# Queries as plain fp32 products, the first head ahead of the rows and the other heads beside them

## The chip, the cores and the metric

The kernel runs on one core of a Trainium2 chip. Its time is device time in microseconds. Before the change the median of three runs is 1752.78 us (1751.76 to 1754.2). A profile is one execution, recorded by the hardware profiler; times inside it are from the start of its span. TensorE, VectorE, ScalarE, Gpsimd and SyncE appear in it as PE (PEld for its weight loads), DVE, ACT, POOL and SP.

## The reference

Two layers over x of 256 tokens and width 1024. Layer 0 mixes tokens by window attention with a gated spatial unit, layer 1 by average pools of four widths. After each mixer stands the part that fills most of the time and that the change touches, a product-key memory of 16384 experts:

```python
q = (xb @ w_q).reshape(n, PEER_HEADS, 2, PEER_DHALF)
s = jnp.einsum('thpk,pnk->thpn', q, sub_keys).astype(jnp.float32)
s_top, i_top = lax.top_k(s, PEER_TOPK)
cand_s = s_top[:, :, 0, :, None] + s_top[:, :, 1, None, :]
cand_i = i_top[:, :, 0, :, None] * PEER_NKEYS + i_top[:, :, 1, None, :]
best_s, best_pos = lax.top_k(cand_s.reshape(n, PEER_HEADS, -1), PEER_TOPK)
idx = jnp.take_along_axis(cand_i.reshape(n, PEER_HEADS, -1), best_pos, axis=-1)
gate = jax.nn.softmax(best_s, axis=-1)
u = jnp.take(down, idx, axis=0)
act = jax.nn.gelu(jnp.einsum('thkd,td->thk', u, xb))
v = jnp.take(up, idx, axis=0)
return jnp.einsum('thk,thkd->td', (gate * act).astype(v.dtype), v)
```

Each token has 8 heads. Per head two query halves of 128 are scored against 128 keys each, the best 16 of each half give 256 sums, and the best 16 of these name 16 experts. Each expert has a row `down` and a row `up` of 1024 floats.

## The kernel before

Channels lie on the 128 partitions in the first part of a layer: `xT` is x transposed, 8 blocks (kb) of 128 channels by 256 tokens. `peer_rows(l)` does the memory of layer l. Its work is cut into 16 **units**: one head for one half of the tokens (128 tokens on the partitions). A unit has 16 **rows**: row k is one gather, a `DMA_INDIRECT` on Gpsimd's queue (L1018) that fetches for each of the 128 tokens its k-th expert, `down` and `up` side by side, 8 KB a token. Rows live in a ring of RING = 12 slots; `fetch` issues a gather when the next slot is free and the unit has been chosen.

Ahead of the rows stand the queries. `norm_split` makes the normed activations in two parts, `xH` (rounded to fp32r) and `xL` (the rest); both, and their sum `hq` made on Gpsimd, occupy three ring slots until the last query. The weights `w_q` come as 16 blocks of 512 KB through a stream of three tiles (`raw`) on SP's queue; each block is split in halves into `sH` (a cast on ScalarE, L105) and `sL` (a subtraction on VectorE, L108). A product is then three fp32r passes, hi by hi, hi by lo and lo by hi (L317 to L319; for head 0, L340 to L343). Two blocks make a head's queries `qT`; `scores` (L1040) multiplies them by the keys, and a copy makes `sc`. `rows_of` turns `hq` into token rows `h2`.

`choose` is the choice of one unit on VectorE, a generator of some 21 steps: top 16 of each half, 256 sums, top 16 of these, expert numbers `eid`, gates by a softmax (Exp on ScalarE). `advance` takes steps of it: 4 after each query block, only for heads before the present one, so that choices stand between the splits of later heads. After the last query the row loop begins: per row a product with `h2`, summed to one number per token (L1102), and 2 steps of choices; per BATCH = 4 rows a Gelu, the gate (`cr`, L1089), four diagonal matrices `dgr` on ScalarE (L1076) and 16 passes on PE that add `up` rows to four banks (L1079). The weights of a batch are made after the first product of the next (`todo`). After its adding a row's slot is free. In layer 0 the loop also multiplies 56 blocks of modulation weights (`md`, 512 KB each, two tiles), one for each fourth row from row 16; they follow `w_q` in the same stream.

When all gathers are out, `after_rows` prepares the pool mixer between the last addings; `pool_shift` sums rows by products with ones, of fp32r parts. Then the residual is added, the pool mixer runs, and layer 1 repeats `peer_rows`. In these parts the order of the code is the order on each engine.

## Time and profile before

| | us |
|---|---|
| median of three runs | 1752.78 |
| profiled execution | 1751.43 |
| its span | 1749.4 |
| PE busy | 1352.9 (77%) |
| DVE busy | 1197.8 (68%) |
| ACT busy | 466.0 (27%) |
| POOL busy | 741.6 (42%) |
| first gather, layer 0 / layer 1 | 236.78 / 1052.56 |
| first product with a row, layer 0 / layer 1 | 269.69 / 1086.74 |
| gathers' share of 16 DMA engines over the span | 74.3% |

The kernel moves 622.52 MB. PE's busy time is modelled from pipelined matmuls, so 77% does not say how near it is to its peak. The granted clock is a share of 2.4 GHz. A stretch tells more than the span: its GB/s, its busy times and its clock say what limits it, and the idle time before an instruction names what ended it.

### The profile page before, as it was taken

Reading aid. Unit: us, or ns where it says so; the run is one execution under the profiler, and the core shown is the slowest. Engines: PE = TensorE matmul, PEld = TensorE weight load, DVE = VectorE, ACT = ScalarE, POOL = GpSimd, SP = SyncE. Lnnn points to the kernel's source line nnn. Section 1 sums busy time; section 2 is a strip of 40 time slices with the busy share of each in tenths; the row PEclk is TensorE's granted clock in tenths of the full one; section 3 lists DMA queues with packets and bytes.
Section 4 is the critical chain, followed back from the end, with each engine's and each line's share of the span. In section 5 each row is a group of like instructions: output and inputs, shape, how many; then the busy total and the mean of one; then the engine's idle time right before and its main releaser. Section 6 shows DMA issues by size and latency. Waiting matters only on the chain. (4 is left out here: it accounts for less than half of the span.)

```text
span 1749.4 us, 15727 instructions
## 1 busy us (share of the span) xinstructions
PE 1352.9 (77%) x4148; PEld 691.8 (40%) x4148; DVE 1197.8 (68%) x2910; ACT 466.0 (27%) x1176; POOL 741.6 (42%) x632
## 2 busy tenths in 40 slices
PE   7988897677767677767777797877877887777776
PEld 3865793233223233223233387333333333333333
DVE  6987768877787776555554377877777775545443
ACT  3555553222222121111111353222222222111112
POOL 3535433443444434444444133544444454544442
PEclk8987998988888978988888899899998898999899
DMA  7434578999999999999999328799999999999993
GB/s 291 164 109 158 170 280 323 419 419 419 418 419 418 419 418 418 419 419 419 419 419 414 135 86 342 321 419 420 419 419 420 419 420 420 420 420 420 418 420 124
DMA packets 97867, 622.52 MB, mean 356 GB/s; under 512 B 11250, under 2 KB 11762, under 8 KB 31860
## 3 DMA queue, kind: packets, MB, share of 16 engines
q0 software_dynamic: 73728, 536.90, 74.3%
q1 hardware_dynamic: 23328, 83.82, 12.9%
q8 instruction: 34, 0.56, 0.1%
q10 hardware_dynamic: 724, 0.80, 0.1%
q14 instruction: 53, 0.43, 0.1%
HBM read 620.44 MB, written 1.05 MB: 355 GB/s over the span
## 5 line engine op out<-in xcount | busy, mean ns | idle before, releaser
L1079 PE MATMUL ps_big<-row,dgr 128*128 128x512 f32 x2048 | 1033.4, 664 | 340.3 <-ACT dgr L1076 340.3
L1018 POOL DMA_INDIRECT row<-in_DU,eid x512 | 609.6, 1191 | 801.7 <-PE ps_big L1079 537.1
L1102 DVE SCALAR_TENSOR_TENSOR row<-row,h 128x1024 f32<-128x1024 f32 x512 | 627.2, 1225 | 419.4 <-DMA row<-in_DU,eid 407.8
L1079 PEld LDWEIGHTS ps_big<-row,dgr 128*128 128x128 f32 x2048 | 424.2, 212 | 948.1 <-issue 504.8
L1076 ACT ACTIVATE dgr<-cf,cr 128x128 f32<-128x128 f32 x512 | 164.0, 390 | 276.9 <-DVE cr L1089 275.2
L1108 ACT ACTIVATE actr<-actr 128x4 f32<-128x4 f32 x128 | 26.3, 205 | 701.0 <-DVE row L1102 700.8
L108 DVE TENSOR_TENSOR sL<-raw,sH 128x512 fp32r<-128x512 f32 x75 | 57.8, 798 | 30.7 <-ACT sH L105 24.9
L884 DVE SCALAR_TENSOR_TENSOR md<-md,crowb 128x1024 f32<-128x1024 f32 x56 | 68.1, 1216 | 0.0
L317 PE MATMUL ps_a<-row,sH 128*128 128x256 f32 x224 | 65.3, 291 | 2.3 <-ACT sH L105 1.4
L318 PE MATMUL ps_a<-row,sH 128*128 128x256 f32 x224 | 63.1, 282 | 1.0 <-issue 1.0
L319 PE MATMUL ps_a<-row,sL 128*128 128x256 f32 x224 | 63.5, 283 | 0.5 <-DVE sL L108 0.4
L105 ACT CAST sH<-raw 128x512 fp32r<-128x512 f32 x84 | 49.2, 619 | 24.5 <-DMA raw<-in_w_q 10.9
L511 PE MATMUL ps_big<-sH,hH 128*128 128x256 f32 x128 | 38.4, 306 | 8.6 <-ACT sH L105 6.1
L317 PEld LDWEIGHTS ps_a<-row,sH 128*128 128x128 f32 x224 | 42.8, 191 | 4.1 <-ACT qTp L1051 2.1
L319 PEld LDWEIGHTS ps_a<-row,sL 128*128 128x128 f32 x224 | 42.7, 191 | 1.7 <-DVE sL L108 1.1
L318 PEld LDWEIGHTS ps_a<-row,sH 128*128 128x128 f32 x224 | 42.8, 191 | 0.7 <-issue 0.7
L1102 DVE DVE_READ_ACCUMULATOR row<-row,h 128x1 f32 x512 | 42.2, 82 | 0.0
L512 PE MATMUL ps_big<-sL,hH 128*128 128x256 f32 x128 | 38.2, 301 | 2.6 <-DVE sL L108 2.5
L1001 ACT ACTIVATE gater<-best,z 128x16 f32<-128x16 f32 x32 | 9.8, 308 | 106.8 <-DVE z L1000 106.7
L513 PE MATMUL ps_big<-sH,hL 128*128 128x256 f32 x128 | 37.2, 296 | 0.1
L1001 ACT ACT_TABLE_LOAD x28 | 35.9, 1283 | 0.5
L1108 ACT ACT_TABLE_LOAD x28 | 35.9, 1283 | 0.4
(265 smaller groups left out, 1315.6 us busy)
## 6 DMA issues: line engine op xcount, KB each, us to landing
md<-in_modT SPq DMA_DIRECT2D x56, 512.0 KB, 7.9
raw<-in_w_q SPq DMA_DIRECT2D x32, 512.0 KB, 3.3
raw<-in_modT SPq DMA_DIRECT2D x19, 512.0 KB, 4.7
row<-in_DU,eid POOLq DMA_INDIRECT x512, 18.5
pro<-in_modT SPq DMA_DIRECT2D x11, 512.0 KB, 3.7
pro<-in_modA SPq DMA_DIRECT2D x8, 512.0 KB, 6.7
raw<-in_in_w SPq DMA_DIRECT2D x8, 512.0 KB, 4.4
pro<-in_in_w SPq DMA_DIRECT2D x6, 512.0 KB
```

Source lines behind the costliest of these rows:

```text
L105: k.nc.scalar.copy(hi, src)
L108: eng.tensor_sub(lo, src, hi)
L317: nc.tensor.matmul(ps, lhsT=hi[:, i], rhs=xh[:, kb], start=(first and i == 0), stop=False)
L318: nc.tensor.matmul(ps, lhsT=hi[:, i], rhs=xl[:, kb], start=False, stop=False)
L319: nc.tensor.matmul(ps, lhsT=lo[:, i], rhs=xh[:, kb], start=False, stop=(last and i == 3))
L884: self.nc.vector.scalar_tensor_tensor(raw, raw, 1.0, crow, op0=OP.mult, op1=OP.mult, accum_out=self.m[:, l, j:j + 1])
L1001: nc.scalar.activation(g, best, AF.Exp, bias=z[:, 0:1], scale=1.0, accum_out=z[:, 1:2])
L1018: nc.gpsimd.indirect_dma_start(r, None, a[f"DU{l}"], bass.IndirectOffsetOnAxis(ap=eid[:, tt, h, k:k + 1], axis=0))
L1076: nc.scalar.activation(dg, self.ident, AF.Copy, scale=cw[:, tt, s:s + 1])
L1079: nc.tensor.matmul(acc[2 * tt + hf], lhsT=dg, rhs=r[:, D + 512 * hf:D + 512 * hf + 512], start=(s == 0), stop=(s == P - 1))
L1102: nc.vector.scalar_tensor_tensor(r[:, :D], r[:, :D], 1.0, h2[:, tt], op0=OP.mult, op1=OP.mult, accum_out=act[:, tt, s:s + 1])
L1108: nc.scalar.activation(act[:, tt, s], act[:, tt, s], AF.Gelu_apprx_tanh)
```

## The change

Queries become plain fp32 products of the unsplit `w_q` tiles with `hq`, which VectorE and ScalarE make directly; a product is two passes on PE. No ring slot is taken for them and the ring has 13 slots. Head 0 is multiplied first, its scores follow, then the queries of head 1; units 0 and 1 are chosen in one piece, with 12 further steps of unit 2, 56 steps in all, ahead of the row loop. Heads 2 to 7 are multiplied in the row loop, two products at every second row (`asks`), and ScalarE's copies of queries and scores are issued one such ask later (`late`). A unit is taken up as soon as its head's scores are there. The `md` blocks have a stream of their own. The last unit's batches are 4, 4, 4, 2, 1, 1. The pool's sums are fp32 products.

```diff
-RING = 12
+RING = 13
...
+    def take(self):
+
+        i = self.pos[0]
+        self.load_ahead()
+        self.pos = (i + 1, 0)
+        return self.raw[i], i
+
+    def give(self, i):
+        self.release(i)
+        self.load_ahead()
...
-    def dense_items(self, l):
...
+    def later_items(self):
+        a = self.a
+        self.pro_end = len(self.st.items)
+        for l in range(2):
+            for j in range(16):
+                self.st.add(a["w_q"][l, j], lambda raw: None)
         for n in range(56):
             lj = (0, 40 + n) if n < 8 else (1, n - 8)
-            st.add(a["modT"][30 + n], lambda raw, lj=lj: self.mod_dot(lj, self.crow)(raw), "md")
-        self.dense_items(1)
+            self.sm.add(a["modT"][30 + n], lambda raw, lj=lj: self.mod_dot(lj, self.crow)(raw), "md")
...
-        st.ahead(4)
-        self.norm_split(self.rin.finish(), self.gcol, self.m[:, l, 24:32], xH, xL, self.xT)
+        st.load_ahead()
+        r = self.rin.finish()
         for kb in range(KB):
-            nc.gpsimd.tensor_add(hq[:, kb], xH[:, kb], xL[:, kb])
+            nc.vector.scalar_tensor_tensor(hq[:, kb], self.xT[:, kb], self.gcol[:, kb:kb + 1], r,
+                                           op0=OP.mult, op1=OP.mult)
+            nc.scalar.activation(hq[:, kb], hq[:, kb], AF.Identity, bias=self.m[:, l, 24 + kb:25 + kb], scale=1.0)
...
-            while steps > 0 and at[0] < len(units) and units[at[0]][1] < ready:
+            while steps > 0 and at[0] < len(units) and units[at[0]][1] in scs:
...
+        def query(ps, w, kb):
+            nc.tensor.matmul(ps[:, :T], lhsT=w[:, kb * P:(kb + 1) * P], rhs=hq[:, kb], start=(kb == 0),
+                             stop=(kb == KB - 1))
+
+        def queries(h):
+
             qT = tk.tile([P, 2, T], F32, name="qTp", bufs=2)
+            late = None
             for p in range(2):
-                ps = first[p] if h == 0 else self.tile_mm(xH, xL)
...
+                ps = self.bank("a")
+                w, i = st.take()
+                for kb in range(KB):
+                    query(ps, w, kb)
+                    if kb == 1 and late:
+                        late()
+                    if kb % 2:
+                        yield
+                st.give(i)
+                late = lambda ps=ps, p=p: nc.scalar.copy(qT[:, p], ps[:, :T])
+            late()
+            yield
+            late = scores(h, qT)
+            yield
+            late()
+
+        qT = tk.tile([P, 2, T], F32, name="qTp", bufs=2)
+        banks = [self.bank("a") for _ in range(2)]
+        blocks = [st.take() for _ in range(2)]
+        for kb in range(KB):
+            for ps, (w, _) in zip(banks, blocks):
+                query(ps, w, kb)
+        for p in range(2):
+            st.give(blocks[p][1])
+            nc.scalar.copy(qT[:, p], banks[p][:, :T])
+        scores(0, qT)()
+        second = queries(1)
+        for tt in range(2):
+            for hf in range(2):
+                rows_of(tt, hf)
+            for _ in range(28):
+                advance(1)
+                if tt == 0:
+                    next(second, None)
+        for _ in second:
+            pass
+        asks = (1 for h in range(2, 8) for _ in queries(h))
...
         for n, (tt, h) in enumerate(units):
             while at[0] <= n:
-                advance(1, 8)
-            for k0 in range(0, 16, BATCH):
-                for k in range(k0, k0 + BATCH):
+                next(asks, 0)
+                advance(1)
+            k0 = 0
+            for m in (BATCH,) * (16 // BATCH) if n < 15 else (BATCH,) * (16 // BATCH - 1) + (2, 1, 1):
+                for k in range(k0, k0 + m):
...
-                    advance(2, 8)
+                    if i % 2 == 0:
+                        next(asks, 0)
+                    advance(2)
...
-            for q in range(2):
-                nc.tensor.matmul(ps, lhsT=self.ones_r, rhs=self.sph[q], start=(q == 0), stop=(q == 1))
+            nc.tensor.matmul(ps, lhsT=self.ones, rhs=self.sp[:, 2 * hf:2 * hf + 2].rearrange("p g e -> p (g e)"),
+                             start=True, stop=True)
```

VectorE at the opening of layer 0, before: `nh` and `row` are the norm and the low part of the activations, `sL` the low parts of weights, `v` and `ix` the first top 16.

```order
L308 SCALAR_TENSOR_TENSOR row<-nh,m,row 128x256
L299 SCALAR_TENSOR_TENSOR nh<-xT,gcol,ps_w 128x256
L308 SCALAR_TENSOR_TENSOR row<-nh,m,row 128x256
L108 TENSOR_TENSOR sL<-raw,sH 128x512 x5
L954 MAX v<-sc 128x8
L956 MAX_INDEX ix<-v,sc 128x8
L958 MATCH_REPLACE wkt<-v,sc 128x128
L960 MAX v<-wkt 128x8
L108 TENSOR_TENSOR sL<-raw,sH 128x512 x2
L962 MAX_INDEX ix<-v,wkt 128x8
L954 MAX v<-sc 128x8
L956 MAX_INDEX ix<-v,sc 128x8
```

And in the changed kernel, from the norm on.

```order
L225 SCALAR_TENSOR_TENSOR ry<-rt_2002,rz 128x2
L932 SCALAR_TENSOR_TENSOR hq<-xT,gcol,ps_w 128x256 x8
L943 MAX v<-sc 128x8
L945 MAX_INDEX ix<-v,sc 128x8
L947 MATCH_REPLACE wkt<-v,sc 128x128
L949 MAX v<-wkt 128x8
L951 MAX_INDEX ix<-v,wkt 128x8
L943 MAX v<-sc 128x8
L945 MAX_INDEX ix<-v,sc 128x8
L947 MATCH_REPLACE wkt<-v,sc 128x128
L949 MAX v<-wkt 128x8
```

The splits are gone from between the steps of the choice, and the norm has 8 instructions.

PE at the end of the queries of layer 0, before: the last fp32r passes, the scores of head 7, and all addings of rows.

```order
L317 MATMUL ps_a<-row,sH 128x256
L318 MATMUL ps_a<-row,sH 128x256
L319 MATMUL ps_a<-row,sL 128x256
L1040 MATMUL ps_w<-keys,qTp 128x128 x4
L1079 MATMUL ps_big<-row,dgr 128x512 x512
```

And now from the first query on: `hq,raw` are queries, `cf,hq` the turning of `hq` into rows, `row,dgr` the addings.

```order
L1039 MATMUL ps_a<-hq,raw 128x256 x16
L1029 MATMUL ps_w<-keys,qTp 128x128 x4
L939 MATMUL ps_a<-cf,hq 128x128 x8
L1039 MATMUL ps_a<-hq,raw 128x256 x16
L1029 MATMUL ps_w<-keys,qTp 128x128 x4
L939 MATMUL ps_a<-cf,hq 128x128 x8
L1039 MATMUL ps_a<-hq,raw 128x256 x4
L1100 MATMUL ps_big<-row,dgr 128x512 x8
L1039 MATMUL ps_a<-hq,raw 128x256 x4
L1100 MATMUL ps_big<-row,dgr 128x512 x8
L1039 MATMUL ps_a<-hq,raw 128x256 x4
```

Queries of heads 2 to 7 stand between the addings, four products after each four rows.

SP's queue from the first w_q load on, before (`md` are modulation blocks).

```order
L70 DMA raw<-in_w_q 128x1024 x16
L70 DMA md<-in_modT 128x1024 x56
L70 DMA raw<-in_w_q 128x1024 x3
L1165 DMA row<-in_pool_w 128x2048
L1169 DMA row<-in_pm 128x1088
```

The same stretch of SP's queue now.

```order
L70 DMA raw<-in_w_q 128x1024 x7
L70 DMA md<-in_modT 128x1024 x2
L70 DMA raw<-in_w_q 128x1024 x2
L70 DMA md<-in_modT 128x1024 x3
L70 DMA raw<-in_w_q 128x1024
L70 DMA md<-in_modT 128x1024 x2
L70 DMA raw<-in_w_q 128x1024
```

Nine of the 16 loads of w_q now stand between loads of md.

## Rows read from the trace of the kernel before

**Rows 1.** The page's strip of GB/s in 40 slices, and its chain by line.

```profile
GB/s 291 164 109 158 170 280 323 419 419 419 418 419 418 419 418 418 419 419 419 419 419 414 135 86 342 321 419 420 419 419 420 419 420 420 420 420 420 418 420 124
...
DMA row<-in_DU,eid 26%; POOL row L1018 3%; DVE row L1102 2%; PE ps_big L1079 2%; DMA raw<-in_w_q 1%; PE ps_big L1226 0%; PE ps_a L317 0%; DVE sL L108 0%; PE ps_a L319 0%; PE ps_a L318 0%; ACT sH L105 0%; PE ps_w L175 0%; PE ps_a L914 0%; PE ps_a L340 0%
```

**Rows 2.** Stretches: length; PE, PEld, DVE, ACT, POOL busy (count); clock, DMA share, GB/s.

```profile
275.00:300.00 25.00, 18.69 (x38) 8.27 (x39) 23.72 (x68) 7.42 (x19) 9.32 (x8) 0.78 0.65 250
340.00:640.00 300.00, 218.93 (x418) 89.47 (x417) 233.42 (x633) 66.53 (x167) 123.59 (x105) 0.86 1.01 419
1080.00:1120.00 40.00, 29.01 (x104) 16.11 (x103) 37.31 (x113) 13.41 (x33) 17.00 (x12) 0.87 0.70 271
1120.00:1660.00 540.00, 422.77 (x855) 173.15 (x854) 364.20 (x914) 115.47 (x317) 256.25 (x214) 0.92 1.01 420
```

**Rows 3.** Gpsimd's timeline: start, us, engine, line, what, [idle before <-releaser].

```profile
236.78 1.17 POOL L1018 DMA_INDIRECT row<-in_DU,eid  x1 [14.27 <-DVE z L1000]
...
268.70 0.94 POOL L1018 DMA_INDIRECT row<-in_DU,eid  x1 [18.62 <-PE ps_a L319]
...
285.37 1.20 POOL L1018 DMA_INDIRECT row<-in_DU,eid  x1 [13.66 <-PE ps_big L1079]
...
1052.56 1.04 POOL L1018 DMA_INDIRECT row<-in_DU,eid  x1 [14.85 <-PE ps_a L319]
...
1102.39 1.24 POOL L1018 DMA_INDIRECT row<-in_DU,eid  x1 [11.69 <-PE ps_big L1079]
```

**Rows 4.** VectorE's timeline, opening of the first layer; last row of the second.

```profile
220.68 0.30 DVE L954 MAX8 v<-sc 128x8 f32<-128x128 f32 x1 [1.55 <-ACT sc L1043]
...
221.88 1.78 DVE L108 TENSOR_TENSOR sL<-raw,sH 128x512 fp32r<-128x512 f32 x2
...
229.31 1.29 DVE L108 TENSOR_TENSOR sL<-raw,sH 128x512 fp32r<-128x512 f32 x2 [1.59 <-ACT sH L105]
...
236.31 0.18 DVE L998 SCALAR_TENSOR_TENSOR eid<-e 128x16 uint32<-128x16 f32 x1
...
269.69 1.21 DVE L1102 SCALAR_TENSOR_TENSOR row<-row,h 128x1024 f32<-128x1024 f32 x1
...
280.66 0.16 DVE L1089 TENSOR_TENSOR cr<-actr,gater 128x4 f32<-128x4 f32 x1 [0.83 <-ACT actr L1108]
...
1723.22 1.23 DVE L1102 SCALAR_TENSOR_TENSOR row<-row,h 128x1024 f32<-128x1024 f32 x1 [1.26 <-DMA row<-in_DU,eid]
```

**Rows 5.** Stretches of the opening, columns as in group 2.

```profile
207.90:210.90 3.00, 2.94 (x14) 2.94 (x14) 2.85 (x7) 1.90 (x6) 0.66 (x1) 0.50 0.03 5
210.90:215.50 4.60, 4.60 (x36) 4.28 (x35) 3.81 (x7) 3.00 (x7) 3.09 (x5) 0.98 0.00 0
```

**Rows 6.** The chain that ended last, 1008 to 1016: start, us, what.

```profile
1010.13 3.58 PE ps_big L1226 x16
```

**Rows 7.** Issues of w_q from 236.5 to 260, and from 1050 to 1130.

```profile
raw<-in_w_q SPq DMA_DIRECT2D x5, 512.0 KB
...
raw<-in_w_q SPq DMA_DIRECT2D x5, 512.0 KB, 9.2
```

**Rows 8.** The page's DMA issues: count, KB each, median us to landing.

```profile
md<-in_modT SPq DMA_DIRECT2D x56, 512.0 KB, 7.9
...
row<-in_DU,eid POOLq DMA_INDIRECT x512, 18.5
```

**Rows 9.** TensorE's timeline, last two groups of rows of each layer.

```profile
977.37 9.66 PE L1079 MATMUL ps_big<-row,dgr 128*128 128x512 f32 x16 [5.46 <-ACT dgr L1076]
989.19 8.83 PE L1079 MATMUL ps_big<-row,dgr 128*128 128x512 f32 x16 [2.16 <-ACT dgr L1076]
...
1717.61 7.13 PE L1079 MATMUL ps_big<-row,dgr 128*128 128x512 f32 x16 [2.85 <-ACT dgr L1076]
1726.65 7.13 PE L1079 MATMUL ps_big<-row,dgr 128*128 128x512 f32 x16 [1.90 <-ACT dgr L1076]
```

**Rows 10.** The gathers' line: min/median/max ns, first and last start.

```profile
L1018 POOL DMA_INDIRECT row<-in_DU,eid x512: 932/942/1994, 236.8 to 1705.6; - x171
```

More of the change, by code (lines that the diff above doesn't have):

```diff
@@ L234, in __init__ @@
         self.p_c = pool("consts", 1)
-        self.p_h = pool("hl", LOOK + 2)
         self.st = Stream(self)
@@ L329, in tile_mm @@
         return ps
-    def pair_mm(self, xh, xl):
-        nc = self.nc
-        banks = [self.bank("a") for _ in range(2)]
-        halves = [self.st.next() for _ in range(4)]
-        for kb in range(KB):
-            e = slice(kb % 4 * P, (kb % 4 + 1) * P)
-            w = [halves[2 * b + kb // 4] for b in range(2)]
-            for (hi, lo), ps in zip(w, banks):
-                nc.tensor.matmul(ps[:, :T], lhsT=hi[:, e], rhs=xh[:, kb], start=(kb == 0), stop=False)
-                nc.tensor.matmul(ps[:, :T], lhsT=lo[:, e], rhs=xh[:, kb], start=False, stop=False)
-            for (hi, lo), ps in zip(w, banks):
-                nc.tensor.matmul(ps[:, :T], lhsT=hi[:, e], rhs=xl[:, kb], start=False, stop=(kb == KB - 1))
-            if kb == 3:
-                self.st.ahead(2)
-        self.st.ahead(LOOK)
-        return banks
     def attention_gmlp(self):
@@ L356, in attention_gmlp @@
         st.rings["pro"] = (pool("ring", 3), 3)
+        self.p_h = pool("hl", LOOK + 2)
         cc = pp.tile([P, KB, 2], F32, name="cc")
@@ L886, in mod_dot @@
         return fn
-    def dense_items(self, l):
-        a, st = self.a, self.st
-        for j in range(16):
-            st.add(a["w_q"][l, j])
-        self.wq_end[l] = len(st.items)
-        if l == 1:
-            return
+    def later_items(self):
[4 more added lines that the diff above has]
+                self.st.add(a["w_q"][l, j], lambda raw: None)
         for n in range(56):
             lj = (0, 40 + n) if n < 8 else (1, n - 8)
-            st.add(a["modT"][30 + n], lambda raw, lj=lj: self.mod_dot(lj, self.crow)(raw), "md")
-        self.dense_items(1)
+            self.sm.add(a["modT"][30 + n], lambda raw, lj=lj: self.mod_dot(lj, self.crow)(raw), "md")
     def residual(self, l, acc, carve):
@@ L1041, in scores, with late @@
                                      start=True, stop=True)
-            sc = tk.tile([P, 2, 2, P], F32, name="sc", bufs=8)
-            nc.scalar.copy(sc, ps.rearrange("p (a b n) -> p a b n", a=2, b=2))
-            scs[h] = sc
-        first = self.pair_mm(xH, xL)
-        for h in range(8):
+            sc = tk.tile([P, 2, 2, P], F32, name="sc", bufs=4)
+            def late():
+                nc.scalar.copy(sc, ps.rearrange("p (a b n) -> p a b n", a=2, b=2))
+                scs[h] = sc
+            return late
@@ L1150, in after_rows @@
                 yield
-        for k in range(12):
+        for k in range(10):
             self.pool_shift(k)
@@ L1186, in pool_columns @@
         yield
-        self.ones_r = self.p_x.tile([P, P], F32R, name="ones_r")
-        nc.scalar.copy(self.ones_r, self.ones)
     def pool_shift(self, k):
@@ L1236, in pool_mixer @@
         self.warm(WARM[1])
-        self.st.ahead(2)
+        self.st.load_ahead()
         self.rin.column()
@@ L1259, in pool_mixer @@
             self.rin.add(self.xT[:, kb])
-        self.st.ahead(4)
         self.dump("x3", self.xT)
```

57 lines of the change are left out of this document (20 added, 37 removed).

## The prediction

> **What bounds the kernel now.** I read the page first: its strip of GB/s stands at about 419 from slice 7 to 20 and 26 to 38, and the chain that ended last is gathered rows for its largest part [rows 1]. So most of the span is two stretches, one a layer, in which 256 gathers (128 rows of 8 KB, 1.049 MB each) pass as fast as the DMA engines take them. The table by stage confirms it: 419 to 420 GB/s for 300 and 540 us, with PE, DVE and ACT far from full [rows 2]. In such a stretch nothing that an engine saves or adds moves the end, as long as it stays under the period of a row: a gather needs 1.049 MB / 420 GB/s = 2.50 us, and VectorE's product of the last row waited for DMA [rows 4]. Time can come only from when the first gather is issued, from holes in the stream after that, from other bytes in it, and from what follows the last row.
>
> The holes stand in the same table: 275 to 300 us in the first layer and 1080 to 1120 in the second [rows 2]. Gpsimd's queue says why. The first gather goes out at 236.78; after the tenth the next waits until 268.70 for a query product, because three of the 12 slots hold the split activations; the thirteenth waits for the first row to be multiplied and added up, 285.37; in the second layer the first goes out at 1052.56 and the thirteenth at 1102.39 [rows 3]. And VectorE shows why the first gather is late: the choice of the first unit is cut by the splitting of weights [rows 4].
>
> **Head start.** The norm chain is the same up to its first instruction, and the first query product can start where it does now, 207.9. Now PE has 48 single passes until 215.5 (14 seen in the first 3.0 us, after a pause, at a granted clock of 0.50, that is 1.2 GHz, and 36 in the next 4.6 at 0.98 [rows 5]). Then it has 32 passes (16 products, two instructions each) of 3.58/16 = 0.22 us at full clock [rows 6]. 3 us at half clock give 7 of them, and 25 x 0.22 = 5.5 us the rest: 216.4 instead of 215.5, about 1 us later. But the scores follow directly: copies of qT, scores and their copy I estimate at 2.3 us (two passes of a copy, 8 score passes of half a query pass each, one copy), 218.7, against 220.68 for the first MAX8 [rows 4], since now the next head's first block and five splits on VectorE stand ahead of it. From MAX8 to the end of eid is 236.31 + 0.18 - 220.68 = 15.8 us, of which 1.78 + 3 x 1.29 are splits (one of the three is shown) and 1.59 a wait for one [rows 4]: 8.6 us remain. Gather one goes out at 218.7 + 8.6 + 0.4 = 227.7 instead of 236.8: **9.1 us**. The second layer has the same sequence; I take the same 9.1. Bounds: if all 32 passes run at half clock, 0.44 each, they take 14 us instead of 8.5 and 3.6 us are left of the 9.1; if none does, 7.0 us, and it is 10.6.
>
> **Holes.** From 275 to 300, 250 of 419 GB/s loses 25 x (1 - 250/419) = 10.1 us; in the second layer 40 x (1 - 271/420) = 14.2 us [rows 2]. Afterwards 13 slots are free at once; 13 gathers are 13 x 2.50 = 32.5 us of transfer. If bytes move some 1.7 us after the first issue (an estimate; the issue itself takes 1), DMA in the second layer has work from 1052.6 - 9.1 + 1.7 = 1045.2 to 1077.7. When does the first slot return? VectorE does units 0 and 1 in full and 13 instructions of unit 2: the first ends at 1043.0, then some 2.7 us until its gate is divided (ScalarE's Exp and its table stand behind the next head's copy), 9.1 for unit 1 and half of that for unit 2: rows start at 1059.3. First product to weighted gates took 280.66 - 269.69 = 11.0 us with the same two steps per row, and 4.7 more to the next gather [rows 3, 4]: 1075.0. That is 2.7 us ahead of the dry point, about what a gather needs to move bytes: I leave 1 us of hole. In the first layer two md tiles and w_q blocks lengthen the cover by some 4 us and there is none. The thirteenth slot is 2.5 us of this cover; once the stream is full it adds nothing. Gain 10.1 + 13.2 = **23.3 us**; bounds 0 (the holes as they are) to 24.3.
>
> **Bytes moved into the stream.** Of 16 w_q blocks 5 are issued after the first gather in each layer now [rows 7]; then seven stand ahead and nine beside rows. Four more, 0.524 MB / 419 GB/s = 1.25 us each: **minus 5.0 us a layer**. The three blocks for layer two that are loaded at the end of layer one stay.
>
> **Tail.** The product of the last row starts at 1723.22 [rows 4], and its four rows' passes on PE end at 1733.8 [rows 9]. With pieces of 2, 1 and 1 the passes of rows 8 to 11 still end at 1717.61 + 7.13 = 1724.7, and 6.9 us for the last four follow without a pause, 1731.6: 2.2 us. In the first layer PE starts both groups after a pause (9.66 and 8.83 us [rows 9]); joined, the second starts at 987.0 and takes 6.9: 993.9 against 998.0, 4.1 us. **6.3 us**; bounds 0 (the last row's own chain through ScalarE sets the end) to 8.
>
> **What I cost at nothing.** Queries beside rows: per four rows PE gets 8 passes, 1.73 us, and a fifth of a head's scores, 0.2, beside 16 row passes of 0.43 (7.13 us [rows 9]): 8.8 us at full clock, against 4 x 2.50 + 0.6 (w_q) = 10.6 us of DMA in the second layer, and 1.25 more with md in the first. The query copies make ScalarE wait for PE; behind them stand the next Gelu and four scalings, and behind these the adding of four rows. But a gather lands 18.5 us after its issue [rows 8], so 7 rows are in flight, and a delay of one group is absorbed. On SP, md loads now stand behind w_q loads that wait for a block's last product; an md tile is wanted 8 rows (22 us) after its load and lands in 7.9 [rows 8]. Without that cover VectorE would wait for md with the rows queued behind. The splits of w_q vanish on VectorE and ScalarE; outside the opening they lay under DMA or PE. The row sums of the pool become two fp32 products, 4 x 0.43 us where four single passes stand, within 1 us either way. The attention part keeps its order up to its last splits.
>
> A rule that speaks against this: VectorE is now dense with choices exactly while Gpsimd issues its 13 gathers. In this trace an issue takes 0.94 us in the median and 1.99 at most, over 512 of them with VectorE 78% busy through much of that time [rows 2, 10]; at 1.99 + 0.30 of gap thirteen take 29.8 us, still under the 32.5 of transfer: no loss. The Trainium skill, "SBUF — State Buffer", section "SBUF: two separate sides", says that Gpsimd cannot write descriptors for its own DMAs while VectorE is in a two-port mode, and in "A bandwidth-pool intuition that's wrong" gives 3100 ns for 620. By that, an estimate of 13 x 3.4 = 44.2 us would be 11.7 us more than the transfer, a layer, and the sum 1738. No issue in this trace is that long, so I go by the row.
>
> **Sum.** First layer 9.1 + 10.1 - 5.0 + 4.1 = 18.3; second 9.1 + 13.2 - 5.0 + 2.2 = 19.5; together 37.8 us. The profiled execution took 1751.4 us (span 1749.4 and 2.0 around it), 1.4 below the median 1752.8; 1751.4 - 37.8 = 1713.6, at the median **1715 us**.
>
> **Rivals.** (1) The hole stays, in part or whole: it turns into a wait for VectorE's choices in place of the one for queries. For it: the margin in the second layer is only 2.7 us, and 56 steps stand ahead of the first row. Against: rows start 25 us earlier than now even so. Each us that the rows start later costs one us a layer: whole holes give 1715 + 23 = 1738, half 1727.
>
> (2) Slower: PE becomes the bound in the some 120 rows a layer that have queries beside them. The granted clock there averages 0.86 and 0.92 [rows 2], that is 72 and 84% of the time at 2.4 GHz, the rest at 1.2, and the half-clock parts follow pauses for ACT. 60 groups of 8.8 us at full clock meet a DMA period of 11.2 on average (10.6 and 11.9); PE decides from a mean clock of 8.8/11.2 = 0.79 down, and the whole gain is gone where a group costs 37.8/60 = 0.63 us more, at 0.74. At 0.70 a group is 12.6 us: 1715 + 60 x 1.4 = 1799. Against it: the queries fill the pauses; in the opening, with PE busy throughout, the clock rose from 0.50 to 0.98 [rows 5]. The Trainium skill, "TensorE: Matmul & The Clock Gate", section "HAM oscillation", has the same direction: gaps bring the half clock, closed gaps remove it; the trace's 0.98 agrees.
>
> (3) Better than forecast: the products of head 0 start warm, no hole in layer two, tail at its upper bound: some 8 to 10 us more, 1706.
>
> **Chances.** Forecast 0.65 (own range 1707 to 1724), rival 1 0.18 (to 1740, the rule on descriptors within it), rival 3 0.08, rival 2 0.07, and 0.02 that terms cancel within 0.2% (3.5 us, about what a measurement tells here from no change). Range 1703 to 1737: it takes in half of the better case and most of rival 1. Faster 0.91, same 0.02, slower 0.07.
>
> **What would show it.** First gather near 227.7, and some 27 us earlier than 1052.56 in the second layer (18.3 of it from the first); no window under 400 GB/s between the second ten us after it and the last row; the first slot's return before the thirteenth gather lands; nine w_q loads beside rows; mean clock in rows not below 0.86; last row to last adding 8 us instead of 10. Wrong if PE has no pause in the rows with queries, if DMA dips after the first 13 gathers, or if the last row lands less than 25 us earlier.

## The result, and the profile after

The changed kernel takes 1713.46 us (median of four runs, 1713.27 to 1717.59) against 1753.49 us in the same comparison: ratio 0.9779, 95% interval 0.9762 to 0.9795. A later group of runs gave 1717.66 against 1749.53, ratio 0.9816 (0.9799 to 0.9834). Differences of a few us between groups are therefore not read from medians below, but from stages of traces. The forecast was 1715 us.

The stages of one execution each, between marks that both traces have: the last transposes of the norm, the first gather, the start of the last row's product, the end of the last adding, the end. The last column is the changed kernel in the later group.

| stage, us | before | after | change | forecast | after, again |
|---|---|---|---|---|---|
| start to norm, layer 0 | 206.4 | 204.4 | -2.0 | 0 | 204.9 |
| norm to first gather | 30.4 | 22.4 | -8.0 | -9.1 | 22.4 |
| first gather to last row | 748.5 | 741.1 | -7.4 | -10.1 + 5.0 | 741.4 |
| last row to last adding | 12.7 | 10.8 | -1.9 | -4.1 | 10.6 |
| to norm, layer 1 | 23.3 | 23.9 | +0.6 | 0 | 23.9 |
| norm to first gather | 31.2 | 22.6 | -8.6 | -9.1 | 22.3 |
| first gather to last row | 670.7 | 662.4 | -8.3 | -13.2 + 5.0 | 663.9 |
| last row to last adding | 10.6 | 8.4 | -2.2 | -2.2 | 8.4 |
| to the end | 15.6 | 15.6 | 0 | 0 | 15.6 |
| span | 1749.4 | 1711.5 | -37.9 | -37.8 | 1713.3 |

The page of the changed kernel, strip of GB/s and chain, answers [rows 1].

```profile
GB/s 294 171 112 143 155 338 415 418 418 419 418 418 418 418 419 419 418 419 419 419 419 419 174 51 413 419 419 419 420 420 420 419 420 420 419 420 421 419 420 128
...
DMA row<-in_DU,eid 60%; PE ps_big L1100 11%; DVE row L1126 3%; PE ps_a L1039 2%; POOL row L1007 1%; PE ps_big L381 1%; PE ps_big L798 1%; DVE dscr L389 0%; ACT dgr L1097 0%; PE ps_big L506 0%; PE ps_w L186 0%; PE ps_big L1247 0%; PE ps_w L789 0%; PE ps_big L504 0%; PE ps_big L505 0%
```

Slices 6 to 21 and 24 to 38, counted from 0, stand at 413 to 421 now, and gathered rows are 60% of the chain instead of 26%. By stretches (columns as in [rows 2]) the kernel before had, in the ten us around its first gather (at 236.78):

```profile
236.00:246.00 10.00, 10.00 (x87) 10.00 (x86) 5.67 (x19) 5.41 (x11) 7.40 (x7) 1.00 0.73 273
```

and the changed kernel, from 0.7 us ahead of its own first gather (226.74) on:

```profile
226.00:236.00 10.00, 3.55 (x15) 2.32 (x13) 7.24 (x32) 3.13 (x6) 7.12 (x8) 0.69 1.01 403
236.00:246.00 10.00, 0.00 (x0) 0.00 (x0) 9.12 (x35) 0.40 (x2) 5.84 (x6) 0.50 1.02 426
256.00:266.00 10.00, 10.00 (x22) 4.76 (x22) 9.90 (x30) 1.48 (x5) 5.05 (x4) 0.78 1.01 409
266.00:276.00 10.00, 10.00 (x29) 5.35 (x29) 9.41 (x28) 4.85 (x11) 5.37 (x5) 1.00 0.99 406
340.00:640.00 300.00, 238.80 (x575) 114.41 (x573) 227.47 (x609) 69.56 (x175) 127.07 (x101) 0.90 1.01 418
950.00:960.00 10.00, 5.49 (x13) 2.09 (x11) 2.70 (x6) 0.21 (x1) 0.00 (x0) 1.00 0.87 360
960.00:970.00 10.00, 7.83 (x13) 3.50 (x14) 5.92 (x17) 6.66 (x20) 5.34 (x4) 0.66 0.05 20
1080.00:1120.00 40.00, 35.92 (x102) 18.20 (x101) 27.84 (x77) 10.12 (x27) 19.63 (x17) 1.00 1.01 419
1120.00:1640.00 520.00, 427.39 (x989) 193.92 (x988) 340.33 (x846) 111.74 (x309) 243.88 (x203) 0.93 1.01 420
```

The first ten us move 403 GB/s instead of 273 (412 instead of 304 when counted from the gather itself), and the holes of 250 and 271 GB/s [rows 2] are gone: the weakest ten us of the first layer before the stream drains at 950 are 262 to 272, at 395. TensorE's clock in the rows is 0.90 and 0.93 of 2.4 GHz. Gpsimd's timeline, first, thirteenth and fourteenth gather of the first layer and the first and fourteenth of the second, answers [rows 3]:

```profile
226.74 1.17 POOL L1007 DMA_INDIRECT row<-in_DU,eid  x1 [26.18 <-PE ps_a L939]
...
243.60 1.19 POOL L1007 DMA_INDIRECT row<-in_DU,eid  x1 [1.56 <-DMA row<-in_DU,eid]
258.79 1.20 POOL L1007 DMA_INDIRECT row<-in_DU,eid  x1 [13.99 <-PE ps_big L1100]
...
1025.14 1.02 POOL L1007 DMA_INDIRECT row<-in_DU,eid  x1 [24.95 <-PE ps_a L939]
...
1056.59 1.60 POOL L1007 DMA_INDIRECT row<-in_DU,eid  x1 [13.32 <-PE ps_big L1100]
```

From first to fourteenth it is 32.0 and 31.5 us, 48.6 and 49.8 from first to thirteenth before. VectorE's opening, answering [rows 4]:

```profile
216.79 0.29 DVE L943 MAX8 v<-sc 128x8 f32<-128x128 f32 x1 [8.72 <-ACT sc L1034]
...
225.66 0.18 DVE L987 SCALAR_TENSOR_TENSOR eid<-e 128x16 uint32<-128x16 f32 x1
...
228.24 0.16 DVE L992 RECIPROCAL z<-z 128x1 f32<-128x1 f32 x1 [2.34 <-ACT gater L990]
...
242.78 1.21 DVE L1126 SCALAR_TENSOR_TENSOR row<-row,h 128x1024 f32<-128x1024 f32 x1
```

From MAX8 to `eid` 9.05 us in one piece, then 2.34 us in which VectorE waits for ScalarE's Exp, and the first product with a row 16.0 us after the first gather. The tail, TensorE's last groups of both layers [rows 9]:

```profile
962.17 16.40 PE L1100 MATMUL ps_big<-row,dgr 128*128 128x512 f32 x32 [6.68 <-ACT dgr L1097]
...
1671.95 7.13 PE L1100 MATMUL ps_big<-row,dgr 128*128 128x512 f32 x16 [2.84 <-ACT dgr L1097]
1681.91 14.00 PE L1100 MATMUL ps_big<-row,dgr 128*128 128x512 f32 x32 [2.83 <-ACT dgr L1097]
```

Two groups run as one here, 32 passes.

### The profile page after: what moved, and what is told of

It reads as the page before. It is cut to its first block, busy times and chain, and to the rows that moved or that the text cites. A ratio compares the mean times of both kernels' runs of the same rounds, so it can differ in the third digit from the quotient of the medians.

```text
span 1711.5 us, 14830 instructions
## 1 busy us (share of the span) xinstructions
PE 1343.8 (79%) x3892; PEld 688.3 (40%) x3892; DVE 1148.1 (67%) x2837; ACT 428.1 (25%) x1113; POOL 728.1 (43%) x607
## 4 chain that ended last, share of the span: by engine, by line
DMA 60%; PE 20%; DVE 12%; issue 4%; ACT 2%; POOL 1%; POOLq 0%; ACTq 0%; SPq 0%; DVEq 0%
DMA row<-in_DU,eid 60%; PE ps_big L1100 11%; DVE row L1126 3%; PE ps_a L1039 2%; POOL row L1007 1%; PE ps_big L381 1%; PE ps_big L798 1%; DVE dscr L389 0%; ACT dgr L1097 0%; PE ps_big L506 0%; PE ps_w L186 0%; PE ps_big L1247 0%; PE ps_w L789 0%; PE ps_big L504 0%; PE ps_big L505 0%
## 5 line engine op out<-in xcount | busy, mean ns | idle before, releaser
L1100 PE MATMUL ps_big<-row,dgr 128*128 128x512 f32 x2048 | 1011.1, 651 | 314.1 <-ACT dgr L1097 314.1
L1134 ACT ACTIVATE actr<-actr 128x4 f32<-128x4 f32 (+1 forms) x132 | 27.0, 205 | 683.5 <-DVE row L1126 683.3
L1039 PE MATMUL ps_a<-hq,raw 128*128 128x256 f32 x512 | 124.5, 392 | 6.8 <-ACT h L940 4.6
L1039 PEld LDWEIGHTS ps_a<-hq,raw 128*128 128x128 f32 x512 | 99.9, 196 | 42.1 <-issue 22.0
L505 PE MATMUL ps_big<-sL,hH 128*128 128x256 f32 x128 | 37.1, 292 | 2.7 <-DVE sL L108 2.7
L943 DVE MAX8 v<-sc 128x8 f32<-128x128 f32 x64 | 18.1, 282 | 25.4 <-ACT sc L1034 25.4
L504 PEld LDWEIGHTS ps_big<-sH,hH 128*128 128x128 f32 x128 | 25.4, 201 | 11.2 <-ACT sH L105 6.3
L766 POOL COPY gate<-mx 128x1 f32<-128x1 f32 x16 | 10.7, 671 | 41.4 <-DVE mx L775 18.2
L789 PE MATMUL ps_w<-dg,p 128*128 128x128 f32 x128 | 22.4, 334 | 6.9 <-DVE mx L776 4.0
L505 PEld LDWEIGHTS ps_big<-sL,hH 128*128 128x128 f32 x128 | 25.2, 197 | 5.0 <-DVE sL L108 4.9
L201 POOL TENSOR_TENSOR row<-row 128x256 f32<-128x256 f32 x12 | 8.7, 727 | 42.4 <-ACT row L197 41.9
```

Of the source, the lines that this page charges most:

```text
L504: nc.tensor.matmul(o, lhsT=hH[b][:, kb, ts], rhs=hi[:, i], start=(kb == 0), stop=False)
L505: nc.tensor.matmul(o, lhsT=hH[b][:, kb, ts], rhs=lo[:, i], start=False, stop=False)
L789: nc.tensor.matmul(pt[:, c * P:(c + 1) * P], lhsT=p[:, c * P:(c + 1) * P], rhs=dg, start=True, stop=True)
L1039: nc.tensor.matmul(ps[:, :T], lhsT=w[:, kb * P:(kb + 1) * P], rhs=hq[:, kb], start=(kb == 0), stop=(kb == KB - 1))
L1100: nc.tensor.matmul(acc[2 * tt + hf], lhsT=dg, rhs=r[:, D + 512 * hf:D + 512 * hf + 512], start=(s == 0), stop=(s == P - 1))
L1134: nc.scalar.activation(act[:, tt, s], act[:, tt, s], AF.Gelu_apprx_tanh)
```

## Experiments

Each is an edit of the changed kernel. "Stream" is the stage from first gather to last row. The first four ran together beside 1751.8 us for the kernel before, the next four beside 1752.4, the last four beside 1749.5.

**e1, the last unit in pieces of 4 again.**

```diff
-            for m in (BATCH,) * (16 // BATCH) if n < 15 else (BATCH,) * (16 // BATCH - 1) + (2, 1, 1):
+            for m in (BATCH,) * (16 // BATCH) if n < 15 else (BATCH,) * (16 // BATCH):
```

> The changed kernel with the last unit's rows in pieces of 4, 4, 4, 4 again instead of 4, 4, 4, 2, 1, 1. Theory A, the prediction's term: the pieces are worth 6.3 us (4.1 in the first layer, 2.2 in the second), so 1713.5 + 6.3 = 1719.8 us. Theory B, read from the two traces: start of the last row's product to the end of the last adding went from 12.7 to 10.8 us in the first layer and from 10.6 to 8.4 in the second, so 4.1 us, 1717.6. Theory C: the last row's own chain through ScalarE sets the end either way, 1713.5.

Measured 1718.51 us, ratio 0.9814 (0.9796 to 0.9833), which cannot tell A from B. The trace can. Last row to last adding is 11.0 us in the first layer (10.8 with the pieces) and 10.6 in the second (8.4). TensorE's timeline at the end of the second (start, length, what, idle time before and what ended it):

```profile
1684.41 7.13 PE L1100 MATMUL ps_big<-row,dgr 128*128 128x512 f32 x16 [1.13 <-ACT dgr L1097]
1693.46 7.13 PE L1100 MATMUL ps_big<-row,dgr 128*128 128x512 f32 x16 [1.92 <-ACT dgr L1097]
```

The two groups stand apart again with 1.92 us between. So the pieces are worth 2.2 us in the second layer, as forecast, and 0.2 in the first: neither A nor B there. The first layer's two groups run as 32 passes without the pieces too. Another 3.0 us of this run came after the last adding (18.6 us instead of 15.6), at a lower clock (last section).

**e2, 12 tiles for rows.** `RING = 12`.

> The changed kernel with 12 tiles for rows instead of 13. Theory A (a tile is 2.5 us of cover until the first slot returns): in the second layer the first gather goes out at 1025.1, bytes move some 1.5 us later, 12 x 2.50 us last until 1056.6, and the first slot returns with the gather at 1056.6, whose bytes move at 1058.2: a hole of about 1.6 us there and none in the first layer, where md and w_q lengthen the cover by some 5 us: 1715 us. Theory B: the thirteenth tile is worth nothing, 1713.5. Theory C: the number of tiles also sets the rate of the full stream; at 420 x 12/13 GB/s in both streams some 100 us more, 1815.

Measured 1715.74, ratio 0.9807 (0.9787 to 0.9827). The first gather behind the slots goes out 32.1 us after the first, as with 13, and the cover is 2.5 us shorter. Stretches of its first layer (columns as in [rows 2]):

```profile
256.00:266.00 10.00, 10.00 (x25) 5.11 (x24) 9.90 (x34) 1.96 (x7) 6.06 (x4) 0.84 0.95 344
266.00:276.00 10.00, 10.00 (x29) 5.17 (x28) 8.28 (x22) 4.45 (x9) 4.79 (x5) 1.00 0.97 394
```

344 and 394 GB/s where the changed kernel has 409 and 406: 2 us, the mechanism of A, but in the first layer, where A saw none. In the second layer the hole that A forecast is there too, with 419 GB/s in the same ten us of the changed kernel:

```profile
1055.00:1065.00 10.00, 10.00 (x28) 5.14 (x28) 9.90 (x35) 2.87 (x10) 5.19 (x5) 1.00 0.88 328
```

The streams are 2.4 and 1.4 us longer than in the first trace of the changed kernel; its later trace has a second stream as long as this one, so of the two only the dips are clear. The last addings of the first layer end 6.4 instead of 10.8 us after the last row, by another fall of the last groups, and take it back. So the thirteenth tile closes a hole of some 2 us in each layer, too little for these times to show. C falls.

**e3, all queries ahead of the rows**, with eight instead of four tiles for scores, which then have to wait longer.

```diff
         asks = (1 for h in range(2, 8) for _ in queries(h))
+        for _ in asks:
+            pass
```

> The changed kernel with the queries and scores of heads 2 to 7 issued ahead of the first row instead of beside the rows; first head, choice, 13 tiles and tail as they are. Theory A (the first slot returns when TensorE gets to the first adding): TensorE has 6 x 32 passes of 0.22 us, 42 us, and the scores to do first, until about 270 and 1070; the first slot returns some 14 to 16 us later than now (258.8 and 1056.6). Against that the blocks that stood beside rows now lengthen the cover by up to 11 us, so the holes are about 0 to 4 us in the first layer and 3 to 8 in the second: 1717 to 1725 us, with the dip in GB/s some 40 us after the first gather. Theory B: the holes go whole to the queries' place beside rows; without it they are as in the kernel before, 10 and 14 us: 1738. Theory C: head start and 13 tiles alone closed them, 1713.5.

Measured 1758.4, ratio 1.0039 (1.0022 to 1.0057): slower than the kernel before, outside all three. The streams are 19.3 and 22.7 us longer. Gpsimd's timeline, thirteenth and fourteenth gather of the first layer:

```profile
246.87 1.41 POOL L1007 DMA_INDIRECT row<-in_DU,eid  x1 [0.52 <-DMA row<-in_DU,eid]
295.80 1.70 POOL L1007 DMA_INDIRECT row<-in_DU,eid  x1 [47.52 <-DVE v L949]
```

It stands still for 48 us. ScalarE's timeline at its end, copy of the last scores, table load and first Gelu:

```profile
289.17 0.59 ACT L1034 COPY sc<-ps_w 128x512 f32<-128x512 f32 x1 [1.02 <-PE ps_w L1029]
...
290.06 1.28 ACT L1136 ACT_TABLE_LOAD   x1
291.35 0.20 ACT L1136 ACTIVATE actr<-actr 128x4 f32<-128x4 f32 x1
```

The Gelu follows the last copy at once. And the waits from 220 to 310 (engine and line, for whom, us in total, times, longest):

```profile
DVE cr L1112 <- ACT actr L1136: 37.1, 1, 37.1
```

The fourteenth gather comes 67.5 us after the first, 35.5 later than now; A had 14 to 16. Its mechanism held (the slots wait for what stands ahead of the first adding), its price did not: six heads took 58.9 us instead of 42 (7.1 of passes and 1.3 of scores each, 8.9 and 8.4 of passes in the first two, and some waits for ScalarE's copies), and ScalarE had the copies of all of them in its queue ahead of the first Gelu, for which VectorE waited 37.1 us. Plain fp32 queries without their place beside the rows lose more than the change wins.

**e4, rows later, and in a second run rows earlier** (11 in place of 40).

```diff
-            for _ in range(28):
+            for _ in range(40):
```

> The changed kernel with 80 instead of 56 steps of the choice ahead of the first row: 24 steps are 1.1 units, about 10 us of VectorE, by which the rows start later. Theory A (the prediction's first rival: each us that the rows start later costs one us a layer once the cover of 13 gathers is used up): in the second layer the margin is about 1 us, in the first some 5, so 9 + 5 = 14 us, 1727, with a dip in GB/s some 35 us after the first gather. Theory B: the margin is nothing and it costs 10 us in each layer, 1733.5. Theory C: the stream does not depend on when rows start, 1713.5.

Measured 1729.69, ratio 0.9871 (0.9854 to 0.9889). The fourteenth gather comes 41.3 and 41.5 us after the first, 9.2 and 10.0 later than now, and the streams are 7.1 and 8.6 us longer. Stretches of the first layer, columns as in [rows 2]:

```profile
225.00:255.00 30.00, 3.97 (x19) 2.73 (x17) 24.73 (x104) 4.03 (x10) 12.76 (x13) 0.57 1.00 412
255.00:280.00 25.00, 16.35 (x39) 8.10 (x40) 20.08 (x44) 6.40 (x19) 9.17 (x7) 0.77 0.71 281
```

The second holds the dip, 281 GB/s. So if a later gather costs one to one once the cover is used up, as A says, the changed kernel has 2.1 and 1.4 us to spare. One delay alone can't show both the margin and the price; e4's second run and e6 give two more points. A is the nearest of the three, and 3.2 us of this run came after the last adding (18.8 instead of 15.6).

> The changed kernel with 22 instead of 56 steps of the choice ahead of the first row, so that only the first unit stands ahead of it and rows start some 14 us earlier. Theory A (the holes are gone, 13 gathers cover the time until the first slot returns, with 1.4 to 2.1 us to spare): nothing to win, 1713.5 us, between 1712 and 1715; slots return earlier while the stream is already full. Theory B (a hole is still hidden in the second ten us): the streams get shorter by 1 to 3 us each, 1709. Theory C (the choices of units 1 and 2 stand between rows now and delay the gathers from the seventeenth on): longer by the wait, 5 us or more, 1719.

Measured 1713.85, ratio 0.9782 (0.9769 to 0.9795). The fourteenth gather goes out nine us sooner after the first and nothing follows: streams 742.1 and 663.1. That gather on Gpsimd (225.2 is the first):

```profile
248.24 1.19 POOL L1007 DMA_INDIRECT row<-in_DU,eid  x1 [3.81 <-PE ps_big L1100]
```

A again: no hole is left to win, and units 1 and 2 are in time between rows too.

**e5, nine blocks of w_q less beside the rows of each layer.**

```diff
-            for j in range(16):
+            for j in range(7):
...
-                w, i = st.take()
+                if 2 * h + p < 7:
+                    kept[0] = st.take()
+                w, i = kept[0]
...
```

> The changed kernel without the nine blocks of w_q that are loaded beside rows in each layer: heads 3 to 7 multiply by the seventh block again, so their queries are not the reference's; every product stays. Theory A (the stream is bound by bytes, 0.524 MB at 419 GB/s = 1.25 us a block, one to one): first gather to last row 11.3 us shorter in each layer, 1713.5 - 22.5 = 1691 us. Theory B: these loads hide in what the gathers leave free, 1713.5. Theory C: with fewer bytes TensorE's groups of 8.9 us at a mean clock of 0.9 bind instead of a period of 10.0, and only half comes back, 1702.

Measured 1695.48, ratio 0.9685 (0.9672 to 0.9699). The streams are 10.6 and 11.0 us shorter, 21.6 of A's 22.5; 3 us went after the second stream (last row to last adding 11.4 instead of 8.4). Bytes go one to one.

**e6, query products twice.**

```diff
-        def query(ps, w, kb):
+        def query(ps, w, kb, times=2):
+            for r in range(times):
...
```

> The changed kernel with each query product of heads 1 to 7 issued twice into the same sum (their queries come out twice as large). Four rows and their queries are then 7.03 + 2 x 1.89 + 0.2 = 11.0 us of TensorE at full clock, against a period of DMA of 11.9 us with md in the first layer and 10.6 in the second. Theory A (closed pauses bring the clock to 1.00): 30 groups of the second layer are 0.4 us over, 12 us, the first layer is unchanged: 1725 us. Theory B (the mean clock stays at 0.90 to 0.93): 12.2 and 11.8 us a group, 0.3 x 30 + 1.2 x 30 = 45 us, 1758. Theory C: rows in flight absorb it all, 1713.5.

Measured 1728.7, ratio 0.9865 (0.985 to 0.988): A's size by another way. By stretches (columns as in [rows 2]):

```profile
226.00:260.00 34.00, 11.63 (x52) 9.41 (x50) 22.98 (x82) 5.77 (x13) 12.02 (x13) 0.69 0.97 394
...
340.00:640.00 300.00, 256.88 (x716) 137.43 (x715) 227.70 (x615) 70.39 (x181) 130.19 (x102) 0.94 1.01 418
1050.00:1080.00 30.00, 13.80 (x34) 7.60 (x35) 28.12 (x89) 5.01 (x15) 6.86 (x5) 0.64 0.84 332
1120.00:1350.00 230.00, 225.15 (x688) 128.40 (x687) 175.09 (x492) 61.60 (x156) 107.45 (x91) 0.99 1.01 419
```

Beside rows TensorE is busy 225 of 230 us at a clock of 0.99, and the stream still stands at 419. What it lost lies in the opening: head 1's doubled queries delay the first rows, the fourteenth gather comes 7.2 and 7.8 us later after the first, and the streams are 6.9 and 7.7 us longer. By e4's rule, with its margins, 5.1 and 6.4 of that are due; the first ten us after the first gather are weaker too, 321 GB/s instead of 412 in the first layer and 313 instead of 343 in the second. With pauses closed the clock rose from 0.96, the changed kernel's in this stretch, to 0.99, and from 0.90 to 0.94 in 340 to 640; B, with the clock left where it was, falls. The Trainium skill, "TensorE: Matmul & The Clock Gate", section "HAM oscillation", says the same of gaps; these rows agree.

**e7, finer pieces at the end, weighted at once.**

```diff
-            for m in (BATCH,) * (16 // BATCH) if n < 15 else (BATCH,) * (16 // BATCH - 1) + (2, 1, 1):
+            for m in (BATCH,) * (16 // BATCH) if n < 15 else (4, 4, 2, 2, 1, 1, 1, 1):
...
                 todo.append((n, k0, m))
                 k0 += m
+                if n == 15 and k0 >= 8:
+                    while todo:
+                        weigh(*todo.popleft())
         nc.scalar.activation(self.small, self.eps, AF.Sqrt, bias=self.eps, scale=0.0)
-        while todo:
-            weigh(*todo.popleft())
```

> The changed kernel with the last unit in pieces of 4, 4, 2, 2, 1, 1, 1, 1, each weighted and added as soon as its Gelu is done, and ScalarE's table for the root after the last scaling. Theory A (what follows the last row is TensorE's backlog of eight rows, 14 us that start too late): with a backlog of one row the end of the last adding comes some 4.5 us after the start of the last row's product, instead of 10.8 and 8.4: 6 + 4 us less, 1703.5. Theory B: more pauses on TensorE bring its half clock in the products that follow (15.6 us from the last adding to the end now, 18.6 in three of the runs above): 3 us of it are given back at the end and as much in the first layer, 1709. Theory C: VectorE waits for ScalarE in each piece and rows are late, no gain, 1713.5.

Measured 1705.99, ratio 0.9742 (0.9729 to 0.9755). TensorE's last groups of both layers:

```profile
969.06 1.98 PE L1100 MATMUL ps_big<-row,dgr 128*128 128x512 f32 x4 [0.52 <-ACT dgr L1097]
971.55 1.98 PE L1100 MATMUL ps_big<-row,dgr 128*128 128x512 f32 x4 [0.51 <-ACT dgr L1097]
...
1665.13 19.43 PE L1100 MATMUL ps_big<-row,dgr 128*128 128x512 f32 x44 [0.71 <-ACT dgr L1097]
1685.06 1.98 PE L1100 MATMUL ps_big<-row,dgr 128*128 128x512 f32 x4 [0.51 <-ACT dgr L1097]
```

One row's four passes are left, and the last adding ends 4.1 and 4.2 us after the start of the last row's product, instead of 10.8 and 8.4: A, 10.9 us in these two stages. The stage to the end took 16.4 instead of 15.6, and between the medians, of two groups of runs, 7.5 us are left. The edit makes the pieces smaller and also issues their weights at once; which of the two won how much was not tried.

**e8, the second layer's first blocks after the first layer's rows.**

```diff
...
         for _ in after:
             pass
+        if l == 0:
+            self.w_q_items(1)
+            self.st.load_ahead(self.nc.scalar)
```

> The changed kernel with the three first blocks of w_q of the second layer loaded after the last adding of the first layer's rows (issued by ScalarE), instead of beside those rows. Theory A (bytes one to one): the first layer's stream is 3 x 1.25 = 3.75 us shorter, 737.4 us from first gather to last row instead of 741.1, the blocks land in the 47 us in which DMA moves 20 to 100 GB/s, and nothing else changes: 1709.7 us. Theory B: the blocks are late for the first product of the second layer's queries, and what is won is lost there: 1713.5. Theory C: the end of the stream is set by what trails the last gathers, not by its bytes, 1713.5 with the first layer's stream at 741.

Measured 1714.95 (1712.74 to 1720.25) against 1717.66 (1714.76 to 1719.88) for the changed kernel beside it, too near for the times to tell. The stages can. The stream is 737.5, as A says to 0.1; but from the last adding to the second norm it takes 26.6 us instead of 23.9, 2.6 longer. ScalarE's timeline there (ACTq is its issuing of DMAs):

```profile
974.86 0.59 ACT L1235 COPY row<-ps_a 128x512 f32<-128x512 f32 x1 [8.10 <-PE ps_a L1233]
975.72 0.59 ACT L1235 COPY row<-ps_a 128x512 f32<-128x512 f32 x1 [0.27 <-PE ps_a L1233]
975.78 1.32 ACTq L70 DMA_DIRECT2D raw<-in_w_q  x3
977.14 0.59 ACT L901 COPY row<-ps_big 128x512 f32<-128x512 f32 x1 [0.84 <-issue]
```

ScalarE issues three DMAs, 1.32 us, between two copies that stand on the path, and TensorE waits 2.10 us for the second instead of 1.17. The larger loss lies in the mixer's first passes behind that, here and in the changed kernel:

```profile
979.46 4.01 PE L1252 MATMUL ps_big<-row,xT 128*128 128x256 f32 x10
...
983.14 2.32 PE L1247 MATMUL ps_big<-row,xT 128*128 128x256 f32 x10
```

The granted clock was 0.83 in the ten us from 974 here and 1.00 in those from 978.5 there, so 1.7 us of the 2.6 lost are TensorE's clock; that the longer wait brought it down fits the order of events but was not tried apart. e10 has the same edit and loses 3.0 in this stage. What was won is mostly lost, but not as B says: the blocks land 4.9 us after issue, long before they are wanted.

**e10, the parts that won, together** (e7, e8, and a pool of two more tiles for w_q: `pool("rq", 2)`, every fourth and fifth block).

> The changed kernel with the finer last unit of the last experiment, the second layer's first blocks of w_q loaded after the first layer's rows, and two more tiles for blocks of w_q (nine instead of seven blocks ahead of the rows). Theory A (each term one to one): 7.5 us as measured for the pieces, 3 x 1.25 us and 2 x 2 x 1.25 us for the blocks: 1713.5 - 7.5 - 3.8 - 5.0 = 1697.2 us. Theory B: the two more blocks a layer delay the first gathers' bytes by what they save beside rows: 1702. Theory C: the terms overlap, and only the pieces count: 1706.

Measured 1697.88, ratio 0.9717 (0.9696 to 0.9738), 19.8 us under the changed kernel beside it, the fastest version of this study that uses all blocks of w_q. Against that one's trace: streams -6.5 and -2.8, last rows to last addings -6.2 and -4.2, last adding to second norm +3.0. The time is A's to 0.7 us, but not term by term: the pieces gave 10.4 instead of 7.5, the blocks loaded between the layers gave their bytes and lost 3.0 again as in e8, and 2.2 us came ahead of the first norm, which the edit leaves alone. That the terms add up, against B and C, the stages show.

**e11, the head start partly undone.** Twelve subtractions between the steps of the first choice, and **the changed kernel again** beside it.

```diff
...
+                if tt == 0 and 2 <= k < 14:
+                    nc.vector.tensor_sub(lo, raw, hi)
```

> The changed kernel with twelve subtractions of 128x512 put between the steps of the first unit's choice, where the kernel before had its splits; their result is not used. One is 0.6 to 0.7 us, 12 are 7.2 to 8.4 us. Theory A (the head start is one to one, and everything behind the first gather follows it): the opening from norm to first gather goes from 22.4 to 30 us in each layer, the streams stay at 741 and 662: 1713.5 + 2 x 7.7 = 1729 us. Theory B (the first rows wait for the choices of units 1 and 2 anyway, the 13 tiles bridge it): only part, 1721. Theory C: the head start does not reach the end, 1713.5.

> The changed kernel unaltered, beside the kernel before and the three others of this group, as their yardstick. All theories: 1713.5 us; up to the last transposes of the attention part (204.4 us in its first trace, 202.8 to 206.1 in the six traces above that have the same instructions there) it varies by some 3 us from one profiled execution to the next, after that by less.

Measured 1732.23, ratio 0.9897 (0.9881 to 0.9913), and 1717.66. The first gather, 28.4 us after the norm at 204.33:

```profile
232.70 1.17 POOL L1007 DMA_INDIRECT row<-in_DU,eid  x1 [32.20 <-DVE z L992]
```

Norm to first gather is 28.4 and 28.0 us instead of 22.4 and 22.3, and the streams, 740.6 and 664.6, are as they were. The size is 6 us instead of 7.7, not 12 x 0.65. VectorE's timeline:

```profile
217.58 0.68 DVE L1082 TENSOR_TENSOR lo<-hq 128x512 fp32r<-128x512 f32 x1
218.18 0.28 DVE L949 MAX8 v<-wkt 128x8 f32<-128x128 f32 x1
218.38 0.67 DVE L1082 TENSOR_TENSOR lo<-hq 128x512 fp32r<-128x512 f32 x1
218.97 0.08 DVE L951 MATCH_VALUE_LOAD ix<-v,wkt 128x8 f32 x1
```

A subtraction takes 0.68, but from one MAX8 to the step after it it is 0.79 with a subtraction between and 0.33 without. So A: 11.7 us, one to one. The span is 17.1 us longer; of the rest, 2.7 lie after the last adding and 1.7 between the last adding and the second norm. The yardstick's time was missed by 4.2 us (1717.66 for 1713.5; the profiled execution took 1715.15, its span 1713.3). Its stages agree with those of the first trace within 0.5 us but for the second stream, 1.5 longer.

## Why the prediction was right

The mechanism is right: an earlier first gather, no hole, four more blocks beside the rows, a shorter tail. That the sum is right to 0.1 us, 37.8 against 37.9, is luck: head start, tail and pool sums fall short by 1.6, 2.2 and 0.6 us, and the holes of the first layer and the stage up to the norm give 2.3 and 2.0 more. Against the later trace the spans differ by 36.1.

- **Head start.** 8.0 and 8.6 us instead of 9.1. The 32 query passes took 8.8 us (8.5 forecast), copies and scores 2.05 (2.3), the choice 9.05 (8.6) and the issue after it 0.9 (0.4). That it reaches the end one to one is e11.
- **Holes.** In the second layer the timing is as forecast: first row 16.1 us after the first gather (15.8), fourteenth gather 31.5 after (31.5). The 1 us of hole that the sum left there did not come: 416 GB/s and more from 1045 to 1085. So -8.3 against -8.2 for that stream is close by chance: the last 20 us ahead of the last row move 248 GB/s instead of 268, 1 us more lost, and the later trace has -6.8. In the first layer the step missed 2.3 us: it counted the hole at 275 to 300 and not what the stream of before lost in its first ten us, 2.7 us at 304 GB/s from the gather on; 0.2 of it remain, and 0.6 are lost at 395 GB/s from 262 to 272. e4 shows the margin (2.1 and 1.4 us where a hole of none and 1 was left), e2 the worth of the thirteenth tile, and e3 that it is the place beside rows which pays.
- **Bytes.** Nine loads beside rows in each layer, 1.25 us each: e5, 1.2.
- **Tail.** 2.2 us in the second layer, as forecast. In the first the step failed: "joined, the second starts at 987.0" had the pieces join the groups, worth 4.1. They join without pieces (e1), start late and partly at half clock (962.17, after 6.68 us of pause; 32 passes in 16.4 us instead of 14.0, clock 0.66 from 960 to 970), and 1.9 us came of it, 0.2 by the pieces.
- **Costed at nothing.** Beside rows TensorE was not the bound, even with twice the query products (e6). The stage with the pool's row sums is 0.6 us longer, within the 1 allowed. The first layer's thirteen gathers start within 16.9 us, with VectorE busy 9.12 of 10 us, and no issue took more than 1.24. The rule of the Trainium skill, "SBUF — State Buffer", section "SBUF: two separate sides", by which the prediction worked out 1738, does not show here; it is for VectorE in a two-port mode, and no row says whether these instructions run in one.
- **Not forecast.** 2.0 us up to the norm. In the traces of this study that stage is 202.7 to 206.1 us in kernels with the same instructions there, and 206.4 before, so I take most of it for chance and count none of it for the change.
- **What was to show it.** First gather 226.7 (227.7), in the second layer 27.4 us earlier (27); last row 35.7 us earlier, where under 25 would have refuted it; clock beside rows 0.90 and 0.93 (not below 0.86); last row to last adding 8.4 us at the end (8). One sign failed as it was worded: "no window under 400 GB/s" up to the last row. From 262 to 272 it is 395, and the last ten us ahead of the last row are far under it, in the kernel before too.
- **Rivals.** The hole that stays: its price fits e4 and most of e6, its condition was missed by 1 to 2 us. TensorE as bound: not reached (e6). The better tail: it was to be had, by e7.

## What to carry to other kernels

When a stream of transfers is the bound, work that must precede the first transfer should be only what names that transfer; on every engine that keeps ahead of the period the rest cost nothing beside the stream here, and full price ahead of it (e11). What it loaded still cost its bytes, one to one (e5). The buffers in flight have to last until the first one returns: count that time through every in-order queue on the way (here ScalarE's copies ahead of a Gelu, 37 us in e3). At the stream's end the batch size is the tail: smaller batches in the last eight rows, weighted at once, took 10.9 us off the two tails and 7.5 off the time.
